# A decoder block's last projection as Strassen products, and raw reloads of plain weight blocks

## The chip, the cores and the metric

The kernel runs on one NeuronCore of a Trainium2 chip. The metric is the device time of one execution in microseconds (us). A core has five engines with queues of their own: TensorE (PE in the profile, with PEld for its weight loads), VectorE (DVE), ScalarE (ACT), GpSimd (POOL) and SyncE (SP), which here only issues DMAs. Each queue is worked off in order; engines wait for each other through semaphores. Matmuls read SBUF and add into PSUM banks of 128 x 512 float32; DVE and ACT read PSUM, POOL is used on SBUF alone.

## The reference: what is computed

One layer of a decoder block on 2048 tokens of width 1024, all in float32 (cut):

```python
h = rms_norm(x, g_norm) * (1 + scale) + shift          # scale, shift, gate from c
proj = h @ w_in                                        # 1024 x 8192
x_rnn, z_rnn, q, k, v, z_attn, g_r, g_a = split(proj)
y_rnn  = (rg_lru(conv(x_rnn)) * silu(z_rnn)) @ w_out_rnn
y_attn = (dilated_attention_mixture(rope(q), rope(k), v) * silu(z_attn)) @ w_out_attn
merged = sigmoid(g_r + b_r) * y_rnn + sigmoid(g_a + b_a) * y_attn
x = x + gate * (merged @ w_o)
return rms_norm(x, g_final)
```

The last projection is `merged @ w_o`, 2048 x 1024 times 1024 x 1024, followed by the residual add and the last norm.

## The kernel before

**Split operands.** Every product in float32 is made of three matmuls in a rounded 32-bit format. An operand is split into a high half (a copy that rounds, `hi_act` on ACT, line 157) and a low half (the difference, `lo_pool` on POOL, line 163, or `lo_dve` on DVE, line 166), and `mm3` (line 151) adds high x high, high x low and low x high. All matmuls stand at line 149; the profile tells them apart by the tile they write.

**The input stage.** Tokens are handled in two halves, f = 0 and 1, of 1024 tokens. For each half the value projections come first, then 28 pairs of weight column blocks, each by Strassen's scheme: a 256-column block of weights (two column tiles, two halves of K: left blocks a11, a12, a21, a22) times 1024 tokens (right operands B11, B21, B22, T1 to T4, each a high and a low tile of 128 x 4 x 512) takes seven products instead of eight. A product is 12 matmuls of 128 x 512 (4 K tiles x 3). In `strassen` (line 347) they go in the order B11, [the last of the pair before], T2, T3, T1, B21, T4, B22, into the PSUM tiles X, Z, W, V, Y. Sums of blocks run through `u1`, `u2`, `u3`. What happens between products is written out by product number: `operand_events` (line 262) loads the four raw blocks to R tiles (five slots), forms sums and differences on DVE and splits seven operands into S tiles (seven slots), each four products ahead (`LEAD`, line 260). In half 0 all 28 x 7 = 196 split operands are also stored to the scratch sD from ACT's DMA queue (line 275), two splits after they are made; in half 1 `load_next` (line 311) reads them back, 512 KB each, seven ahead. The whole stage is in program order.

**Pools.** Tiles of a stage lie in a pool; when a pool is closed and the next opened at its place, a new tile waits for those that lay where it lies. `rp` holds the tiles of the recurrent branch, of gates and of plain pairs, `qp` those of the last six pairs with the rotary turn; `xp` those with which the next half's operands are prepared meanwhile (`next_norm`, `next_even`, lines 1274 and 1297; `build`, line 514, makes one K tile of a right operand with a work tile hf). `rotary_tables` (line 1005) computes sine and cosine tables in some 18 small DVE steps, one after each product from `TABLES` on, and the four pieces at `PIECES`.

**Attention and output projections.** From about 1411 us on attention runs head by head, and its gaps are filled with steps of the two branch projections. `steps` (line 1708) is a generator of eight jobs: four token blocks of 512 through w_out_rnn, then four through w_out_attn. A job has 8 tiles (128 output rows), a tile 8 steps, a step three matmuls into a pj tile (two PSUM buffers). Within a tile stand the load of the next weight blocks (`load_w`, from split weights in the scratch wD, or, after `whole` is set, raw and split at once), the eviction of the tile before (`evict`: times the sigmoid gate on DVE from PSUM, for the attention jobs plus the other branch's part, line 1770 and 1772), the loads of its gate blocks into fg tiles (four slots), the store to mrT or meT, and in the last tile of a job the loads and splits of the next job's eight y blocks (`load_y`, `split_y`; blocks 1 to 4 through four R tiles). Six jobs are run inside the stretch written out in program order (line 1866); jobs 6 and 7, the ones that need the last heads, follow after it.

**The last projection.** There the program's planner sets the order, from its own estimate. Job 6's 64 steps come first in program text; then `output_operands` (line 1879) loads w_o, multiplies it by the residual gate and splits it into oh and ol; then `output(n)` (line 1887) for each block of 128 tokens loads x and merged (mraw), splits merged (mh, ml), makes 2 x 24 matmuls into pq tiles, adds x, squares and scales the row and stores it, one DMA of 512 KB. Between the blocks eight steps of job 7 are placed.

Of the kernel before, what the change touches and what calls it, by code (L numbers as in the profile page):

```python
# [10 lines left out]
F32 = mybir.dt.float32  # L11
# [15 lines left out]
H = 8  # L27
# [11 lines left out]
TABLES = 24  # L39
PIECES = (56, 76, 91, 111)  # L40
# [49 lines left out]
def decoder_block(ctx, tc, x, c, positions, g_norm, w_mod, b_mod, w_in, b_gate, conv_w, conv_b,  # L90
# [239 lines left out]


# [15 lines left out]
    def strassen(up, f, key, done):  # L347

        x = pair_id[key]
        if f and x == 0:  # L350
            while n_loaded[0] < NS:
                load_next()
        n_op = iter(range(7 * x, 7 * x + 7))
# [7 lines left out]
        def prod(ps, b, first, last, op=None):  # L361
# [6 lines left out]
            if f:  # L368
                used.add(i)
                while n_loaded[0] - NS in used:  # L370
                    load_next()
            run_late(n_prod[0])
# [138 lines left out]
    def n_hf(st):  # L511
        return 1 if st is xp else 2

    def build(st, names, xs, k, first=False, keep=None, pt=None):
# [7 lines left out]
        if keep is not None or first:  # L522
            hf = keep if keep is not None else T(st, [P, CH], F32, "hf", bufs=n_hf(st))[:]
# [5 lines left out]
        else:  # L529
            hf = T(st, [P, CH], F32, "hf", bufs=n_hf(st))  # L530
# [318 lines left out]
    def second_values():  # L849
# [5 lines left out]
        for i in range(4):  # L855
# [8 lines left out]
            plan[7, i].append(lambda i=i: [load_next() for _ in range(4 if i == 0 else 1)])  # L864
        plan[1, 0].append(lambda: ss.append(squares(x3)))
# [139 lines left out]
    def rotary_tables(rp, f):  # L1005
# [70 lines left out]
        at_, base = TABLES, n_prod[0]  # L1076
        for fn in (angles, None, products, *reduce(TWO_PI * 4096, 7, 8), *reduce(TWO_PI, 11, 5), quarter, sines):
            if fn:
                after_prod.setdefault(base + at_, []).append(fn)
            at_ += 1  # L1080
# [216 lines left out]
    def next_even():  # L1297
# [4 lines left out]
        def make(k):  # L1302
            if k % KH == 0:
                operand("B21" if k else "B11")
            build(xp, ("B11", "B21"), x0, k, pt=px.pop(k))
# [9 lines left out]


# [4 lines left out]
    for f in range(2):  # L1321
# [8 lines left out]
        rp = pools.open("rp", bufs=1)  # L1330
        plain_pool[0] = rp
# [21 lines left out]
        touch = [T(qp, [P, CH], F32, tag, bufs=n) for tag, n in (("t0", NT0), ("t1", NT1), ("u1", 1), ("u2", 2), ("u3", 1))]  # L1353
# [351 lines left out]
    stored, whole = set(), []  # L1705


    def steps(jobs):
# [4 lines left out]
        def load_w(x):  # L1713

            if x < 2 * len(tiles):
                assert x == n_w[0]
                j, m = tiles[x // 2]
                if not whole:
# [3 lines left out]
                n_w[0] += 1  # L1722
                W[x] = T(pS, [P, 2, KH, P], F32R, f"S{x % 4}")
                t = T(whole[0], [P, KH, P], F32, "wr", bufs=3)
                rows = slice(x % 2 * KH * P, (x % 2 + 1) * KH * P)
                nc.sync.dma_start(t[:], (w_out_rnn, w_out_attn)[jobs[j][0]][0, rows, m * P : (m + 1) * P]
# [225 lines left out]
```

## Time and profile before

| | |
|---|---|
| median of three runs | 2271.21 us (2270.94 to 2274.93) |
| the profiled execution | 2274.52 us, its span 2272.7 us |
| busy, share of the span | PE 98%, PEld 82%, DVE 61%, ACT 54%, POOL 44% |
| input stage, half 1 (838 to 1411 us) | PE 572.7 of 573.0 us busy |
| from job 6's first matmul to the end | 1989.6 to 2272.7 us |

The span is what the profile covers, from the first to the last instruction; the execution's own time has a little around it. A group of instructions is listed as line, engine, operation, output <- inputs by tile names, shapes and count, then busy us and mean ns of one, then idle time before them and what ended it. A matmul's own length in such a row (about 390 ns) is longer than the distance between two starts, since matmuls are pipelined; the cost per matmul is therefore read from the distance of starts.

### The profile page before, as it was taken

The page shows a single profiled execution, that of the slowest core. Times are in us where ns is not written, and L with a number is a line of the kernel's source. Part 1 is how long each engine was busy: PE and PEld are TensorE (multiplying, and loading weights), DVE is VectorE, ACT ScalarE, POOL GpSimd, SP SyncE. Part 2 cuts the span into 40 slices and gives each one's busy share as a digit, 9 for nine tenths or more (in the row PEclk, how much of TensorE's full clock was granted, in tenths as well). Part 3 has the DMA queues.
Part 4 walks back from the last instruction along what each step waited for, and adds up shares of the span by engine and source line. Part 5 has one row for each costly group of instructions (what it writes and reads, how often), then busy time and mean ns, then how long its engine had stood idle before and what let it go on. Part 6 is the DMA issues. An engine that isn't in the chain of part 4 may idle for free.

```text
span 2272.7 us, 34029 instructions
## 1 busy us (share of the span) xinstructions
PE 2220.0 (98%) x11454; PEld 1864.4 (82%) x11455; DVE 1382.2 (61%) x2384; ACT 1230.5 (54%) x2397; POOL 990.9 (44%) x738
## 2 busy tenths in 40 slices
PE   8999999999998999999999999999999999989998
PEld 5997788888777997888888887888889898868887
DVE  5568887767557465544444343466677878666443
ACT  3546777667542436655556411567778877533211
POOL 2268677766566343212222111456566666332100
PEclk9999999999999999999999999999999999999999
DMA  8366887887998448887887999989988897898542
GB/s 281 89 200 244 278 299 251 291 279 248 305 302 262 153 146 288 271 272 265 278 271 256 303 328 328 284 271 270 283 273 264 233 277 230 251 322 270 155 131 91
DMA packets 429011, 573.40 MB, mean 252 GB/s; under 512 B 72134, under 2 KB 293026, under 8 KB 427812
## 3 DMA queue, kind: packets, MB, share of 16 engines
q1 hardware_dynamic: 390996, 451.47, 64.4%
q10 hardware_dynamic: 37648, 119.70, 13.7%
q8 instruction: 91, 1.49, 0.3%
q14 instruction: 84, 0.69, 0.1%
q0 software_dynamic: 192, 0.05, 0.0%
HBM read 357.18 MB, written 213.91 MB: 251 GB/s over the span
## 4 chain that ended last, share of the span: by engine, by line
PE 59%; DMA 6%; DVE 3%; ACT 2%; SPq 2%; issue 1%; POOL 1%; ACTq 0%; POOLq 0%; DVEq 0%
PE pj L149 12%; PE X L149 8%; PE pq L149 8%; PE V L149 8%; PE W L149 4%; PE Z L149 4%; PE sc L149 4%; PE o L149 4%; PE Y L149 3%; DMA R<-in_w_in_dram 2%; PE pT L1555 1%; PE pg L149 1%; PE pT L1568 1%; DMA R<-yaT 1%; SPq L252 1%
## 5 line engine op out<-in xcount | busy, mean ns | idle before, releaser
L149 PE MATMUL pj<-yh,S 128*128 128x512 f32 x1024 | 344.7, 397 | 9.0 <-ACT S L157 5.3
L149 PE MATMUL V<-T,S 128*128 128x512 f32 x1344 | 332.6, 396 | 5.8 <-DVE t L449 2.6
L149 PE MATMUL X<-T,S 128*128 128x512 f32 x1344 | 332.6, 396 | 3.7 <-ACT u L382 1.9
L163 POOL TENSOR_TENSOR S<-R,S 128x512 fp32r<-128x512 f32 x168 | 252.7, 1512 | 166.8 <-ACT S L157 145.6
L149 PEld LDWEIGHTS V<-T,S 128*128 128x128 f32 x1344 | 253.4, 189 | 66.9 <-DVE ev L449 2.7
L149 PEld LDWEIGHTS X<-T,S 128*128 128x128 f32 x1344 | 254.0, 189 | 64.9 <-ACT u L382 2.4
L149 PEld LDWEIGHTS pj<-yh,S 128*128 128x128 f32 x1024 | 194.4, 190 | 49.8 <-ACT S L157 6.1
L149 PE MATMUL pj<-yl,S 128*128 128x512 f32 x512 | 202.3, 395 | 2.1 <-DVE yl L166 1.1
L163 POOL TENSOR_TENSOR S<-s,S 128x512 fp32r<-128x512 f32 x84 | 131.3, 1564 | 128.6 <-ACT S L157 95.5
L1471 ACT ACTIVATE pp<-pp,st 128x256 f32<-128x256 f32 (+3 forms) x256 | 133.4, 523 | 74.4 <-DVE st L1470 74.1
L149 PE MATMUL Y<-T,S 128*128 128x512 f32 x672 | 166.5, 397 | 0.0
L149 PE MATMUL W<-T,S 128*128 128x512 f32 x672 | 165.8, 395 | 0.0
L149 PE MATMUL Z<-T,S 128*128 128x512 f32 x672 | 165.8, 395 | 0.0
L163 POOL TENSOR_TENSOR s<-R,s 128x512 fp32r<-128x512 f32 x32 | 43.9, 1372 | 250.2 <-ACT s L157 205.8
L149 PEld LDWEIGHTS Y<-T,S 128*128 128x128 f32 x672 | 127.3, 190 | 29.7
L149 PEld LDWEIGHTS W<-T,S 128*128 128x128 f32 x672 | 126.0, 188 | 29.9 <-DMA kT<-t 0.9
L149 PEld LDWEIGHTS Z<-T,S 128*128 128x128 f32 x672 | 126.3, 188 | 29.4
L166 DVE TENSOR_TENSOR ptl<-pT,pth 128x384 fp32r<-128x384 f32 (+1 forms) x160 | 97.8, 628 | 51.1 <-ACT pth L157 48.9
L944 DVE SCALAR_TENSOR_TENSOR xc<-xr,par,xc 128x512 f32<-128x512 f32 x96 | 96.1, 1001 | 50.0 <-ACT xc L938 47.8
L1470 DVE CUSTOM_DVE_ANT_0 pp<-sc,msk 128x256 f32<-128x256 f32 (+3 forms) x256 | 104.2, 449 | 36.3 <-PE sc L149 34.1
L1535 ACT ACTIVATE pp<-pp,M 128x256 f32<-128x256 f32 (+3 forms) x256 | 118.1, 524 | 9.2 <-DVE M L1659 9.2
L163 POOL TENSOR_TENSOR kq<-kraw,kq 128x512 fp32r<-128x512 f32 (+1 forms) x64 | 101.2, 1592 | 41.7 <-ACT kq L157 32.1
(333 smaller groups left out, 4767.7 us busy)
## 6 DMA issues: line engine op xcount, KB each, us to landing
sD<-S ACTq DMA_DIRECT2D x196, 512.0 KB, 4.0
S<-sD SPq DMA_DIRECT2D x196, 512.0 KB, 4.8
S<-wD SPq DMA_DIRECT2D x99, 512.0 KB, 6.3
R<-in_w_in_dram SPq DMA_DIRECT2D x136, 256.0 KB, 4.0
wD<-s ACTq DMA_DIRECT2D x64, 256.0 KB, 4.9
T<-in_w_mod_dram SPq DMA_DIRECT2D x8, 1024.0 KB, 12.1
vN<-ev SPq DMA_DIRECT2D x64, 128.0 KB, 2.0
zaT<-ev SPq DMA_DIRECT2D x32, 256.0 KB, 4.6
```

What stands on the lines that cost most here:

```text
L149: nc.tensor.matmul(o, lhsT=l, rhs=r, start=st, stop=sp, **kw)
L163: nc.gpsimd.tensor_tensor(o, i, h.bitcast(F32), ALU.subtract)
L166: nc.vector.tensor_tensor(o, i, h.bitcast(F32), ALU.subtract)
L252: nc.sync.dma_start(t[:, :, o : o + src.shape[1]], src[half * KH * P : (half + 1) * KH * P].rearrange("(k p) m -> p k m", p=P))
L944: nc.vector.scalar_tensor_tensor(xc, xr[:, i : i + CH], cw(i), xc, ALU.mult, ALU.add)
L1470: nc.vector.tensor_tensor_reduce(pdst, s_ps, mask, 1.0, 3e38, ALU.add, ALU.min, m_)
L1471: nc.scalar.activation(pdst, pdst, AF.Exp, bias=m_, scale=-1.0, accum_out=l_)
L1535: nc.scalar.activation(pp, pp, AF.Copy, scale=w)
L1555: nc.tensor.transpose(pt[:, c0 + j * P : c0 + (j + 1) * P], pp[i][:, k * P : (k + 1) * P], ident)
L1568: nc.tensor.transpose(pt[:, c * P : (c + 1) * P], pp[:, half * P : (half + 1) * P], ident)
```

## The change

1. **The last projection by seven products.** `output_products` takes the place of `output_operands` and `output`. The right operands B11, B21, B22, T1 to T4 are made of the gated w_o: w_o comes in K tiles, and for each of four K indices a `group` of 2 gate products, 4 differences and 3 low halves on DVE, 7 high halves on ACT and 4 low halves on POOL is placed at numbered steps of jobs 6 and 7. The left side is merged, two 128-token blocks at a time (eight pairs): four raw loads from meT, four sums or differences, seven splits, issued `LEAD` products ahead, with S and R slots that jobs 6 and 7 leave. Evictions add into the x rows, partly on POOL (`add_x`), squares and scaling go in halves of 512 columns, one and two products later.
2. **Jobs 6 and 7 in program order.** All of it now lies inside the stretch in program order. Weight blocks from number 99 (`RAW_W`) on come raw into three slots, loaded four half tiles ahead (`u + 4`) and split two ahead (`split_w`); y blocks 5 to 7 of both jobs go through R tiles and are loaded in the first steps of the last tile before; the store of a tile is issued at step 5 instead of 7.
3. **Plain left blocks not stored.** The operands 0, 4 and 5 of a pair are the blocks a11, a12 and a22 themselves. For the 26 pairs whose columns come in fewer than 8 pieces they are no longer stored to sD; in half 1 they are loaded raw (256 KB) and split again, ACT and POOL, four products ahead (`split_next`).
4. **Placing in the input stage.** The table steps are spread, two to seven products, from product 32 on, the pieces later; `touch` claims the u tiles first in `rp` and `qp`, so that they lie at the same place in both; the work tile of `build` in `next_even` is one of three t1 tiles instead of a single hf.

```diff
-TABLES = 24
-PIECES = (56, 76, 91, 111)
+TABLES = 32
+PIECES = (117, 124, 131, 138)
...
+    PLAIN = {0: (0, 0), 4: (0, 1), 5: (1, 1)}
+    loaders, unsplit = {}, []
...
+        if len(pieces) < H:
+            loaders[x] = load
...
-            kept.append((7 * x + i, t))
+            if i not in PLAIN or x not in loaders:
+                kept.append((7 * x + i, t))
...
-            nc.sync.dma_start(t[:].bitcast(F32), sD[n])
+            if n % 7 in PLAIN and n // 7 in loaders:
+                unsplit.append((n, t, loaders[n // 7](*PLAIN[n % 7])))
+            else:
+                nc.sync.dma_start(t[:].bitcast(F32), sD[n])
...
+    def split_next(n):
+        while unsplit and unsplit[0][0] <= n:
+            _, t, r = unsplit.pop(0)
+            hi_act(t[:, 0], r)
+            lo_pool(t[:, 1], r, t[:, 0])
...
-            hf = T(st, [P, CH], F32, "hf", bufs=n_hf(st))
+            hf = T(st, [P, CH], F32, "hf", bufs=2) if st is vx else T(st, [P, CH], F32, "t1", bufs=NT1)
...
-                after_prod.setdefault(base + at_, []).append(fn)
-            at_ += 1
+                after_prod.setdefault(base + TABLES + 7 * (x // 2) + 2 * (x % 2), []).append(fn)
...
+        touch(rp, (("u1", 1), ("u2", 2), ("u3", 1), ("xc", 2), ("y", 2), ("gi", 1), ("a", 1), ("t", 1)))
...
+        touch(qp, (("u1", 1), ("u2", 2), ("u3", 1), ("t0", NT0), ("t1", NT1)))
...
+        def split_w(x):
+            if RAW_W <= x < 2 * len(tiles):
+                t = raw_w.pop(x)[:]
                 W[x] = T(pS, [P, 2, KH, P], F32R, f"S{x % 4}")
+                hi_act(W[x][:, 0], t)
+                (lo_dve if x % 2 else lo_pool)(W[x][:, 1], t, W[x][:, 0])
...
-                if k in (1, 2, 3, 4):
+                if k in (1, 2, 3, 4) or j >= LAST_HEAD and k:
                     load_yd(ys, n, k)
...
+                u = 2 * t + k // KH
                 if k % KH == 1:
-                    load_w(2 * t + k // KH + 3)
+                    for x in range(n_w[0], min(u + (4 if u + 3 < RAW_W else 5), 2 * len(tiles))):
+                        load_w(x)
+                    split_w(u + 2)
...
-                if k == 7 and t:
+                if k == (7 if j < LAST_HEAD else 5) and t:
                     store(t - 1)
...
+            return ((0, gate(0)), (1, gate(1)), (3, hi("B11", b11)), (4, hi("B22", b22)), (4, sub(t3, b22, b12)),
+                    (5, lo("B11", b11, lo_pool)), (6, hi("T3", t3)), (7, lo("B22", b22, lo_pool)),
+                    (7, sub(b12, b12, b11)), (9, hi("T1", b12)), (9, lo("T3", t3, lo_pool)), (10, sub(b22, b22, b12)),
+                    (11, hi("B21", b21)), (12, lo("T1", b12, lo_dve)), (13, hi("T2", b22)),
+                    (13, lo("B21", b21, lo_pool)), (16, lo("T2", b22, lo_dve)), (18, sub(b21, b21, b22)),
+                    (20, hi("T4", b21)), (22, lo("T4", b21, lo_dve)))
...
+        for k, (a, b, g) in enumerate(((4, 7, 16), (20, 30, 42), (40, 64, 72), (69, 85, 94))):
+            at_step(a, lambda k=k: load_o(k))
+            at_step(b, lambda k=k: load_o(KH + k))
+            at_step(g, lambda k=k, g=g: [at_step(g + d, fn) for d, fn in group(k)])
...
+        for x in range(len(order)):
+            X = T(pf, [P, CH], F32, "X", bufs=2)
+            product(X, "B11", True, False, 7 * x)
+            while held:
+                held.pop()()
+            Z = T(pf, [P, CH], F32, "Z")
+            product(Z, "T2", True, True, 7 * x + 1)
+            u1 = T(gp, [P, CH], F32, "u1", bufs=1)
+            u2 = T(gp, [P, CH], F32, "u2", bufs=2)
+            nc.scalar.activation(u1[:], X[:], AF.Copy)
+            tt(u2[:], Z[:], u1[:], ALU.add)
+            add_x(x, 0, 1, u2)
+            Wp = T(pf, [P, CH], F32, "W")
+            product(Wp, "T3", True, True, 7 * x + 2)
+            u3 = T(gp, [P, CH], F32, "u3", bufs=1)
+            tt(u3[:], Wp[:], u2[:], ALU.add)
+            add_x(x, 1, 1, u3)
+            add_x(x, 1, 0, u3)
+            V = T(pf, [P, CH], F32, "V")
+            product(V, "T1", True, False, 7 * x + 3)
+            finish(x, 1, 1, V, u3)
+            product(X, "B21", False, True, 7 * x + 4)
+            finish(x, 0, 0, X, None)
+            Y = T(pf, [P, CH], F32, "Y")
+            product(Y, "T4", True, True, 7 * x + 5)
+            finish(x, 1, 0, Y, u3)
...
-    spend(fill, KT * KT, 0)
-    output_operands()
-
-    for n in range(NB):
-        for _ in output(n):
-            for _ in range(KT):
-                next(fill, None)
+        pools.close("ap", "sc", "pT", "po")
+        output_products(fill)
```

More of the change, by code (lines that the diff above doesn't have):

```diff
@@ L522, in build @@
         if keep is not None or first:
[L523 removed]
+            hf = keep if keep is not None else T(st, [P, CH], F32, "hf", bufs=2)[:]
             if keep is None or k < KH:
@@ L1717, in load_w @@
                 j, m = tiles[x // 2]
-                if not whole:
+                if x < RAW_W:
                     load_wd(jobs[j][0], m, x % 2)
```

220 lines of the change are left out of this document (162 added, 58 removed).

## The prediction

> **What bounds the kernel now.** I read the page first, then the stages of the last 283 us, the chain in order of time, and what TensorE (PE) waited for.
>
> ```profile
> span 2272.7 us, 34029 instructions
> PE 2220.0 (98%) x11454; PEld 1864.4 (82%) x11455; DVE 1382.2 (61%) x2384; ACT 1230.5 (54%) x2397; POOL 990.9 (44%) x738
> ```
>
> PE is busy for 98% of the span, so time is won only by fewer matmuls or fewer waits of PE. The stages, columns as in the view (length, then busy us and instructions of PE, its weight loads, DVE, ACT, POOL, then granted clock, DMA share, GB/s); the first row counts only matmuls into pj:
>
> ```profile
> 1411.00:1989.60 578.60, 286.16 (x1152) 210.19 (x1153) 32.13 (x47) 1.00 0.87 264
> ```
> ```profile
> 838.00:1411.00 573.00, 572.69 (x2466) 462.17 (x2467) 258.30 (x358) 268.51 (x407) 126.51 (x96) 1.00 0.87 285
> ...
> 1989.60:2009.20 19.60, 11.71 (x37) 8.49 (x35) 5.94 (x8) 3.04 (x5) 2.54 (x2) 0.82 1.00 326
> 2009.20:2264.50 255.30, 255.23 (x1116) 210.43 (x1116) 131.90 (x214) 66.68 (x105) 39.60 (x21) 0.99 0.60 188
> 2264.50:2272.70 8.20, 0.00 (x0) 0.00 (x0) 2.91 (x8) 1.35 (x3) 0.00 (x0) 0.73 0.16 64
> ```
>
> Six of the eight projection jobs have 6 x 192 = 1152 matmuls, so the two last ones start at 1989.6. From there to the end are 283.1 us: 384 matmuls of jobs 6 and 7 (counted from 0) and 768 of the last projection, 1152 in all. What one costs, from the chain in order of time (start, length, what):
>
> ```profile
> 1364.65 2.79 PE Y L149 x12
> ...
> 2079.37 10.89 PE pq L149 x48
> 2090.26 5.45 PE pj L149 x24
> ```
>
> 48 in 10.89 and 24 in 5.45 are 0.227 us each; in the input stage's products 12 take 2.79, or 0.2325. So the 283.1 us are 1152 x 0.227 = 261.5 of PE work, 8.2 behind the last matmul, and 13.4 lost, nearly all between 1989.6 and 2009.2 (37 matmuls, 8.4 us of work, in 19.6).
>
> What PE waited for, the rows that matter here (us in total, times, longest):
>
> ```profile
> PE pj L149 <- ACT S L157: 5.3, 1, 5.3
> PE pg L508 <- DVE hf L531: 4.3, 2, 2.6
> ...
> PE pj L149 <- ACT yh L157: 2.6, 1, 2.6
> PE V L149 <- DVE t L449: 2.6, 3, 1.8
> ...
> PE V L149 <- DVE ev L449: 2.3, 1, 2.3
> PE X L149 <- ACT u L382: 1.9, 1, 1.9
> ...
> PE X L149 <- DMA S<-sD: 1.8, 2, 1.5
> ```
>
> **The last projection.** Sixteen row blocks times 48 matmuls become eight pairs times seven products of 12: 672 instead of 768. The time of a product lies between 12 x 0.227 = 2.72 and 2.79. I take 2.79, because that row is the same instruction pattern (a split block stationary, a four-part right operand moving): 56 x 2.79 = 156.2 instead of 768 x 0.227 = 174.3, a gain of 18.1 (21.8 at the other end).
>
> The other engines must keep up with that. Durations from the groups by line and shape (after the bar: busy us, mean ns of one), first of the whole run, then of the stretch from 1990 on:
>
> ```profile
> L163 POOL TENSOR_TENSOR S<-R,S 128x512 fp32r<-128x512 f32 x168 | 252.7, 1512 | 166.8 <-ACT S L157 145.6 <-DMA R<-in_w_in_dram 8.4 <-issue 6.3
> ...
> L157 ACT ACTIVATE S<-R 128x512 fp32r<-128x512 f32 x168 | 102.1, 620 | 20.2 <-DMA R<-in_w_in_dram 12.2 <-DVE R L292 3.5 <-DMA kT<-t 2.5
> ...
> L283 DVE TENSOR_TENSOR s<-R,R 128x512 f32<-128x512 f32 x28 | 32.6, 1163 | 10.5 <-DMA qT<-t 6.9 <-DMA R<-in_w_in_dram 3.6
> ```
> ```profile
> L163 POOL TENSOR_TENSOR S<-wr,S 128x512 fp32r<-128x512 f32 x14 | 24.3, 1737 | 81.2 <-ACT S L157 72.7 <-DMA wr<-in_w_out_attn_dram 8.5
> ...
> L1910 DVE SCALAR_TENSOR_TENSOR ob<-xo,ss,gf 128x1024 f32<-128x1024 f32 x16 | 20.6, 1284 | 0.6
> L1908 ACT ACTIVATE ob<-xo 128x1024 f32<-128x1024 f32 x16 | 16.8, 1050 | 28.7 <-DVE xo L1905 27.8 <-DMA out_dram<-ob 0.8
> ...
> L1772 DVE TENSOR_TENSOR fg<-fg,fg 128x512 f32<-128x512 f32 x17 | 16.2, 953 | 1.1 <-DMA fg<-mrT 1.0
> ...
> L166 DVE TENSOR_TENSOR S<-wr,S 128x512 fp32r<-128x512 f32 x15 | 13.4, 894 | 5.4 <-ACT S L157 5.3
> L1770 DVE TENSOR_TENSOR fg<-pj,fg 128x512 f32<-128x512 f32 x17 | 11.7, 687 | 9.6 <-PE pj L149 8.1 <-DMA mraw<-meT 0.8 <-DMA fg<-gaT 0.7
> ...
> L1883 DVE TENSOR_TENSOR xo<-xo,gate_b 128x1024 f32<-128x1024 f32 x8 | 10.3, 1301 | 1.9 <-DMA xo<-in_w_o_dram 1.8
> ```
>
> Per pair (19.5 us of PE): POOL 7 low halves and 3 adds of x, 10 x 1.51 = 15.1; DVE 4 sums x 1.16, 6 PSUM adds x 0.69, 4 half-width scalings x 0.64 and some 2 us of one-column steps, 13.4; ACT 7 x 0.62 and about 4 more. Each fits. POOL's adds wait for u2 and u3, so for PE, and the splits behind them wait with them; but a split is queued four products (11 us) ahead. I take 2 us for the first pair, whose x rows and fifth to seventh split slots come only after job 7's memory is free (0 to 8).
>
> **Jobs 6 and 7 in program order.** PE work stays 384 x 0.227 = 87.2. Counting what DVE and POOL get in these 87 us. DVE: 16 evictions x (0.687 + 0.953) = 26.2; 20 low halves of weights and y x 0.894 = 17.9; four operand groups, each two gate products, four differences and three low halves, 4 x (2.6 + 4.65 + 2.68) = 39.7; three sums for the first pair, 3.5: 87.3 in all. POOL: 14 weight low halves x 1.737 and 24 others x 1.512, 60.6. The groups start at step 16 of 128; before it stand some 11 us of work, so 137 fall into the remaining 76.2 us of PE, 90 per 50 us. Have they ever gone so densely? The busiest 50 us of the input stage:
>
> ```profile
> 200.00:250.00 50.00, 47.70 (x198) 37.70 (x197) 45.06 (x49) 36.15 (x58) 34.60 (x23) 0.97 0.70 250
> 250.00:300.00 50.00, 50.00 (x217) 40.55 (x216) 41.54 (x53) 37.30 (x61) 36.68 (x25) 1.00 0.86 287
> ...
> 600.00:650.00 50.00, 48.05 (x201) 38.60 (x200) 15.04 (x24) 15.22 (x27) 20.56 (x15) 0.97 1.00 304
> ```
>
> DVE and POOL together reach 78.2 per 50 with PE always busy, and 79.7 with PE waiting 2.3. At 78.2 the 137 take 87.6 us, 11.4 too many. PE tolerates an eviction one tile late (5.4 us, two PSUM buffers), but of that the gate load eats some 2: it is issued 3.4 us before its tile ends and lands after
>
> ```profile
> meT<-fg SPq DMA_DIRECT2D x9, 256.0 KB, 5.5
> fg<-gaT SPq DMA_DIRECT2D x9, 256.0 KB, 5.1
> fg<-mrT SPq DMA_DIRECT2D x8, 256.0 KB, 5.6
> ```
>
> leaving 3.2. So 8 us of PE waiting, and 2 more because everything is queued in program order (a high half on ACT that waits for a late DVE difference holds up the next weight block behind it): 10. The lower end is 0: DVE's 87.3 alone just fit. The upper end, from rows of undisturbed and disturbed lengths (min/median/max ns):
>
> ```profile
> L163 POOL TENSOR_TENSOR S<-wr,S x14: 1278/1682/2347, 2010.1 to 2142.8; 128x512 fp32r<-128x512 f32 x14
> ```
> ```profile
> L166 DVE TENSOR_TENSOR S<-wr,S x15: 677/693/1785, 2009.2 to 2145.5; 128x512 fp32r<-128x512 f32 x15
> ```
>
> The same DVE subtraction lasts 0.68 or 1.79, and 1.79 is 0.68 and most of one POOL subtraction: where both read two SBUF operands, one stands while the other runs. If that is complete, their undisturbed lengths add up: 36 on POOL x 1.278 = 46.0, 34 on DVE x 0.677 = 23.0, groups 4 x (2 x 1.3 + 7 x 0.677) = 29.4: 98.4 for 76.2, less 3.2: 19.0. I keep 10, by the row of 250 to 300, which is the nearest mixture. The Trainium skill, page "SBUF — State Buffer", section "Who interferes with whom", says that a VectorE instruction with two SBUF inputs and a GpSimd one that reads SBUF exclude each other for a whole instruction. The trace agrees in kind (1.79 against 0.68); by the rule to the letter the sum would have 19.0 here.
>
> A second road to the same wait are the transfers. The four fg buffers turn in load 5.6, add 1.0, store 5.5 and issues 0.5, 12.6 us for two tiles that PE does in 10.9; SP stands at the load that needs the slot, and the next weight load stands behind it. That the store is issued two steps earlier gives back 1.4. And the bytes: 29 raw weight blocks, 32 gate blocks, 16 stores, 10 y blocks and 4 left blocks of 0.26 MB, with 4.7 of w_o and its gate, are 28.6 MB; the stage from 1989.6 moved 326 GB/s at a full DMA share, which makes 88 us of it. Both lie inside the same 0 to 19 and are not added.
>
> **The start of job 6.** Today it loses 11.2 us: y blocks loaded late (2.6), the first raw weight block split late (5.3), the rest half clock. Now y 5 to 7 are loaded in job 5's last tile, and a raw block is loaded four half tiles ahead (10.9 us) and split two ahead. The y loads still wait for the slots of y 1 and 2, so I leave 2 us (0 to 11).
>
> **The end.** 8.2 becomes 7.5: square and scaling go at half width (0.5 of the 1.05 saved; the two scalings still follow each other), and the last store is 256 KB (bounds 6.5 and 8.2).
>
> **The front.** In the stage of 838 to 1411 the 78 plain blocks (26 pairs, three each) come raw, 256 instead of 512 KB, and cost 78 x 0.62 on ACT and 78 x 1.51 on POOL: ACT goes to 317 and POOL to 244 of 573 us, both covered by PE. An ACT high half waits for its load, and PSUM copies queue behind it; it is queued three products (8.4 us) after the load, which takes
>
> ```profile
> S<-sD SPq DMA_DIRECT2D x196, 512.0 KB, 4.8
> ...
> R<-in_w_in_dram SPq DMA_DIRECT2D x136, 256.0 KB, 4.0
> ```
>
> so 0, at most 5. In the first half 78 stores of 512 KB go; the rest are issued later, since two kept blocks stay behind, and the worst (block 3) only two products, 5.6 us, before its slot is written again, against 4.0 to landing:
>
> ```profile
> sD<-S ACTq DMA_DIRECT2D x196, 512.0 KB, 4.0
> ```
>
> 0, at most 3, ACT standing. The stalls named above: DVE's table steps, one per product (the 2.3 at V, half clock after it: 0.97 over 50 us is 1.5), are spread over seven products for every two: 3.8. The u copy that stood behind a store of the closed pool,
>
> ```profile
> 619.03 0.60 ACT L382 ACTIVATE u<-X 128x512 f32<-128x512 f32 x1 [7.94 <-DMA gaT<-ev]
> ```
>
> now gets a u tile's place: 1.9 and half clock (0.97 in the row of 600 to 650 above), 3.4. Of the 4.3 at hf (three buffers instead of one) I take 2, since ACT stood behind late loads there too; of V behind t 1, of S from sD 1.2. Minus 0.4 for new waits: 11 (3 to 17). What is late next near 619 and 659 are the many-piece loads of the rotated blocks, which stay.
>
> **The sum.** From 1989.6: 87.2 + 2 + 10 + 156.2 + 2 + 7.5 = 264.9 against 283.1, 18.2 less; with 11 in front 29.2 less: span 2243.5. The profiled execution took 2274.52 with a span of 2272.7, the median is 2271.21; so 1.5 below the span, 2242.
>
> **Rivals.** (1) DVE and POOL keep up in jobs 6 and 7 because part of the lag is worked off in the product phase: stall 0, 2232. For it: DVE alone fits. Against: 90 per 50 us has no precedent. (2) They exclude each other fully: 19.0 instead of 10, 2251. (3) Slower: POOL becomes the bound of the product phase. Its 15.1 us per pair are synchronised with PE twice (u2, u3); if a pair took it 24 us instead of 19.5, eight pairs would add 36, 2278. It decides from 23.2 us per pair (29.2 / 8 above 19.5). Against: between u3 and the next u2 lie six products, 16.7 us, for eight POOL operations of 12 us.
>
> **Numbers.** Forecast 0.47, rival 1 0.27, rival 2 0.18, rival 3 0.06, no change 0.02 (0.2%, 4.5 us, is about what a measurement tells). Best ends (stall 0, 2.72, front 17) give 2222; rival 2 with the front at 3 gives 2259, with late first pairs 2262. Range 2222 to 2262. Faster 0.92, same 0.02, slower 0.06.
>
> **What would show it.** 672 matmuls into X, Z, W, V, Y after job 7, 2.79 a product; PE waits in jobs 6 and 7 on DVE's fg or the weight halves, about 10 us, with DVE over 90% busy there; no PE wait behind u at line 382 near 619. Wrong if PE waits on S or POOL in the product phase, or on S in the second half of the input stage.

## The result, and the profile after

| | before | after |
|---|---|---|
| median | 2273.36 us (9 runs) | 2280.71 us (9 runs) |
| ratio | | 1.0036, 95% interval 1.0023 to 1.0049 |
| profiled execution, its span | 2274.52, 2272.7 us | 2277.73, 2275.7 us |

The change made the kernel 0.36% slower; 1.3% faster was forecast. From the page of the changed kernel:

```profile
span 2275.7 us, 34368 instructions
PE 2210.1 (97%) x11358; PEld 1848.6 (81%) x11359; DVE 1485.9 (65%) x2472; ACT 1301.8 (57%) x2575; POOL 1223.6 (54%) x908
```

The 96 matmuls are gone and PE is busy for 9.9 us less, yet the span is 3.0 us longer. The stages of the changed kernel from the end of the input stage on (same columns as in the prediction): attention with jobs 0 to 5, jobs 6 and 7, the products, and what lies behind the last matmul.

```profile
1400.20:1977.20 577.00, 564.88 (x3553) 502.06 (x3552) 398.01 (x1101) 409.91 (x1093) 324.33 (x279) 1.00 0.87 266
1977.20:2090.00 112.80, 96.62 (x386) 73.80 (x385) 90.97 (x93) 40.80 (x70) 58.96 (x38) 0.95 0.88 264
2090.00:2266.20 176.20, 163.38 (x672) 129.91 (x671) 125.36 (x206) 59.30 (x139) 109.71 (x78) 0.96 0.44 138
2266.20:2275.70 9.50, 0.42 (x2) 0.00 (x0) 5.24 (x17) 0.93 (x3) 0.00 (x0) 0.65 0.29 110
```

Job 6 starts at 1977.2, where it started at 1989.6: 12.4 us are won in front, 11 were forecast. Against the sum of the prediction, the loss in jobs 6 and 7 is 112.8 - 87.2 = 25.6 instead of 12 (13.6 more), the products take 176.2 instead of 158.2 (18.0 more), the end 9.5 instead of 7.5 (2.0 more); with 1.4 more won in front that makes the 32.2 us between 2243.5 and 2275.7. What PE waited for (us in total, times, longest), first in jobs 6 and 7, then in the product phase:

```profile
PE pj L149 <- DVE S L166: 4.0, 5, 1.5
PE pj L149 <- DMA S<-wD: 3.1, 1, 3.1
PE pj L149 <- DVE yl L166: 2.9, 3, 1.8
PE pj L149 <- DVE fg L1794: 2.5, 2, 1.5
PE pj L149 <- POOL yl L163: 1.4, 1, 1.4
...
```
```profile
PE V L149 <- DVE xo L2000: 12.8, 8, 2.4
```

In the product phase there is one wait only: for V, the PSUM tile that the last product of a pair leaves to DVE's add into the x rows (line 2000). The order of time shows it in a long pair and in the short one behind it (start, length, what, idle before):

```profile
2115.65 2.96 PE L149 MATMUL W<-F,S 128*128 128x512 f32 x12
2121.02 4.46 PE L149 MATMUL V<-F,S 128*128 128x512 f32 x12 [2.42 <-DVE xo L2000]
...
2139.29 2.96 PE L149 MATMUL W<-F,S 128*128 128x512 f32 x12
2143.16 3.04 PE L149 MATMUL V<-F,S 128*128 128x512 f32 x12 [0.90 <-DVE xo L2000]
```

A wait of 2.42 us is followed by half clock here all four times (granted clock 0.50 from 2123 to 2125 us; 4.46 instead of 3.04 for twelve matmuls), one of 0.90 is not, and so the pairs alternate: by the starts of Z, 20.1, 23.6, 20.6, 23.6 us and so on. It is no fixed rule: in copies_no_gates, one of the runs below, a wait of 2.58 us leaves the granted clock at 1.00. And what DVE itself waited for in these 176.2 us, the four costliest:

```profile
DVE ss L2013 <- ACT jk L2011: 19.7, 15, 1.9
DVE xo L2000 <- POOL xo L2032: 9.7, 8, 1.4
DVE s L1944 <- DMA R<-meT: 7.7, 1, 7.7
DVE u L2045 <- ACT u L2044: 5.3, 7, 0.8
```

DVE is busy for 125.4 us and stands for 42.4 more at these four, which is 95% of the stage: it hardly ever waits for PE. The 7.7 are a single wait, at the first pair's raw blocks; the others come back with every pair. Its queue is a closed chain of work and of waits for ACT and POOL, and PE runs at that chain's pace.

### The profile page after: what moved, and what is told of

Same layout as the page of the kernel before. It is cut to its first block, busy times and chain, and to the rows that moved or that the text cites. A ratio compares the mean times of both kernels' runs of the same rounds, so it can differ in the third digit from the quotient of the medians.

```text
span 2275.7 us, 34368 instructions
## 1 busy us (share of the span) xinstructions
PE 2210.1 (97%) x11358; PEld 1848.6 (81%) x11359; DVE 1485.9 (65%) x2472; ACT 1301.8 (57%) x2575; POOL 1223.6 (54%) x908
## 5 line engine op out<-in xcount | busy, mean ns | idle before, releaser
L163 POOL TENSOR_TENSOR S<-R,S 128x512 fp32r<-128x512 f32 x278 | 412.7, 1491 | 364.8 <-ACT S L157 318.7
L157 ACT ACTIVATE S<-R 128x512 fp32r<-128x512 f32 x278 | 170.7, 622 | 137.0 <-DMA R<-in_w_in_dram 91.3
L163 POOL TENSOR_TENSOR S<-s,S 128x512 fp32r<-128x512 f32 x112 | 165.9, 1481 | 131.8 <-ACT S L157 99.1
L149 PEld LDWEIGHTS Z<-T,S 128*128 128x128 f32 x672 | 126.6, 188 | 29.7
L149 PEld LDWEIGHTS Y<-T,S 128*128 128x128 f32 x672 | 126.6, 188 | 29.3
L157 ACT ACTIVATE S<-s 128x512 fp32r<-128x512 f32 x117 | 73.0, 624 | 126.4 <-issue 33.4
L1489 DVE CUSTOM_DVE_ANT_0 pp<-sc,msk 128x256 f32<-128x256 f32 (+3 forms) x256 | 104.1, 448 | 36.4 <-PE sc L149 34.2
```

Source lines behind the costliest of these rows:

```text
L149: nc.tensor.matmul(o, lhsT=l, rhs=r, start=st, stop=sp, **kw)
L157: nc.scalar.activation(o, i, AF.Copy)
L163: nc.gpsimd.tensor_tensor(o, i, h.bitcast(F32), ALU.subtract)
L1489: nc.vector.tensor_tensor_reduce(pdst, s_ps, mask, 1.0, 3e38, ALU.add, ALU.min, m_)
```

## The product phase: order, and what DVE and POOL keep from each other

**V in two banks.** Is it the single bank of V, or the chain?

```diff
-            V = T(pf, [P, CH], F32, "V")
+            V = T(pf, [P, CH], F32, "V") if x % 2 == 0 else T(pj, [P, CH], F32, "pj")
```

> The changed kernel; the V tiles of the odd pairs take the PSUM bank that job 7 leaves (a tile named pj), so that two V tiles exist at a time. In the changed kernel PE waits 12.8 us, eight times, at V for the add into xo (line 2000), and four of these waits are followed by half clock; the phase from 2090.0 to 2266.2 takes 176.2 us where 56 products are 156.2. Theory A (order): DVE has time enough, the add only stands behind norm steps in its queue, and one bank is all that makes PE feel it: the waits go, the pairs take 19.6 us each, the phase 156 to 159, the kernel 18 to 20 us less than the changed one. Theory B (throughput): DVE and POOL together need 20.6 us or more per pair; the wait only moves, to Z, X or a split operand S, and the phase stays above 165, the gain under 11 us.

Measured: 2280.29 us, ratio to before 1.0035 (1.0021 to 1.0048), the same as without the edit. All pairs from the second on are 22.1 to 22.2 us apart; after's mean is 176.2 / 8 = 22.0. What PE waits for has moved:

```profile
PE X L149 <- ACT u L2044: 10.0, 7, 1.5
PE pj L149 <- DVE xo L2000: 3.4, 4, 1.1
PE V L149 <- DVE xo L2000: 2.3, 3, 0.8
```

```profile
2087.90:2262.60 174.70, 159.06 (x673) 125.03 (x671) 125.22 (x206) 59.20 (x139) 109.58 (x78) 1.00 0.45 139
```

The half clock is gone (granted clock 1.00 in the phase), and the phase is 1.5 us shorter, no more. So neither the bank nor the half clock is the cause; theory A falls as it was put, and the chain has a period of 22.1 us.

**Adds first.** The seven calls that put the next operands' work on the queues go behind the adds of each product:

```diff
             done_n[0] += 1
-            run_jobs(done_n[0])
...
             finish(x, 1, 1, V, u3)
+            run_jobs(done_n[0])
```

> The changed kernel; in the product phase the adds behind a product (into u or xo) are put on the queues ahead of the next operands' sums and splits and of the norm steps, which were ahead of them. V stays one bank. Theory A (order): the add into xo that frees V then runs some 2 us behind the last product of a pair, 3 us before V is wanted, and u3 and POOL's adds of x come earlier as well: the phase takes 156 to 160 us instead of 176.2, the kernel 16 to 20 us less than the changed one. Theory B (throughput of DVE and POOL): the operands come late instead, PE waits on S, and the phase stays above 165.

Measured: 2267.72 us, 0.9976 (0.9965 to 0.9988). The phase, and what DVE waited for most in it:

```profile
2091.50:2256.30 164.80, 158.16 (x673) 125.23 (x672) 126.59 (x204) 57.55 (x138) 106.78 (x78) 1.00 0.48 148
```
```profile
DVE ss L2012 <- ACT jk L2010: 17.2, 7, 2.5
DVE s L1945 <- POOL S L163: 7.1, 6, 1.2
```

The phase is 164.8 us, the pairs 21.0 from the third on: 11 of the 20 lost us were order alone. That lies between the two theories, above A's 156 to 160 and just under B's 165. The waits of DVE for POOL's add of x and for ACT's copy are gone from its list; left are the two shown.

**Fewer low halves on POOL.**

```diff
                 hi_act(t[:, 0], v[name])
-                lo_pool(t[:, 1], v[name], t[:, 0])
+                (lo_pool if i % 2 else lo_dve)(t[:, 1], v[name], t[:, 0])
```

> The kernel with the adds ahead (evict_first: pairs of 21.0 us, phase 164.8), and in the product phase four of a pair's seven low halves (operands 0, 2, 4, 6) on DVE instead of POOL. Theory A (DVE and POOL exclude each other while both read two SBUF operands, and that sum is the limit): per pair 10 POOL operations x 1.28 and 8 such DVE operations x 0.68 are 18.2 us of 19.5, and a low half costs 1.28 on POOL but 0.68 on DVE, so four moved leave 15.8: pairs of 19.6 to 20.0, the phase 157 to 160. Theory B (DVE's own queue is the limit): DVE, busy for 15.8 us a pair, gets 2.7 more, and the pairs stay at 21 or grow, the phase 165 or more.

Measured: 2263.71 us, 0.9959 (0.9944 to 0.9973). The stage:

```profile
2094.90:2253.20 158.30, 156.42 (x673) 125.95 (x672) 138.19 (x237) 57.66 (x139) 72.35 (x47) 1.00 0.49 155
```

158.3 us, which is what the prediction had for it (158.2). DVE got 31 operations of 0.68 more, 21 us, and is busy for only 11.6 more than with the adds first alone (138.2 against 126.6 in 164.8): its other operations became shorter by the rest (the sum at line 1944, for one, 0.68 us on average instead of 1.21). Theory A's numbers hold, B falls. What the run doesn't separate is POOL's lateness: with the adds first alone DVE waited 7.1 us and PE 1.8 for a low half from POOL, and these waits are gone too. Where the prediction's "some 2 us of one-column steps" went shows in the groups of the changed kernel's product phase (busy us, mean ns of one) and, for the step at line 176, in its order of time behind POOL's last instruction:

```profile
L176 DVE TENSOR_TENSOR ss<-ss 128x1 f32<-128x1 f32 x14 | 15.1, 1076 | 0.5
...
L177 DVE TENSOR_TENSOR ss<-ss 128x1 f32<-128x1 f32 x14 | 9.6, 688 | 0.5
...
L170 DVE TENSOR_SCALAR ss<-ss 128x1 f32<-128x1 f32 x14 | 2.2, 154 | 0.5
```
```profile
2267.46 0.16 DVE L176 TENSOR_TENSOR ss<-ss 128x1 f32<-128x1 f32 x1
...
2268.23 1.41 DVE L2020 SCALAR_TENSOR_TENSOR xo<-xo,ss,gf 128x512 f32<-128x512 f32 x2
```

The step at line 176 takes 0.16 us where POOL is idle and 1.08 on average in the phase, that at line 177 0.69. Both multiply two columns from SBUF. The steps with one column as input (lines 170, 175 and 178) take 0.15 us every time. Line 179 also has two, and takes 0.16: POOL is idle when it runs (in the first long pair POOL's last low half ends at 2118.43 us and line 179 begins at 2118.67). All seven kinds of one-column steps together take 42.9 us, some 5 a pair.

## Jobs 6 and 7: two losses that add

**POOL's low halves as copies on ACT** (weights, y and the four of a group that are POOL's; `lo_copy` is a copy by ACT):

```diff
-                (lo_dve if x % 2 else lo_pool)(W[x][:, 1], t, W[x][:, 0])
+                (lo_dve if x % 2 else lo_copy)(W[x][:, 1], t, W[x][:, 0])
```

> The changed kernel with the 38 low halves that POOL makes in jobs 6 and 7 (weights, y, operand groups) replaced by copies on ACT: these low halves are not computed. DVE keeps every instruction. From job 6's first matmul to job 7's last the changed kernel takes 112.8 us for 87.2 of PE work; DVE is busy for 91.0 of it, and its subtractions last 0.68 or 1.77 us. Theory A (DVE and POOL exclude each other): all of DVE's subtractions fall to 0.68, DVE's busy time to about 74, and the 25.6 lost us to 5 to 9, of which some 4.4 are the late weight block at the start. Theory B (the order of the queues, or the transfers): DVE's durations fall but PE still waits for fg and S, and 18 or more are still lost. Theory C (DVE's own work alone is too much): also 18 or more lost, with DVE busy over 85.

Measured: 2270.46 us (one execution). The same DVE subtraction in the changed kernel and here, ns min/median/max:

```profile
L166 DVE TENSOR_TENSOR F<-wo,F x12: 679/1766/1785, 2005.9 to 2083.8; 128x512 fp32r<-128x512 f32 x12
```
```profile
L166 DVE TENSOR_TENSOR F<-wo,F x12: 683/685/1781, 2005.5 to 2076.5; 128x512 fp32r<-128x512 f32 x12
```

and the stretch:

```profile
1978.40:2082.50 104.10, 94.68 (x385) 75.57 (x384) 64.44 (x92) 58.01 (x105) 3.41 (x3) 0.93 0.93 284
```

With POOL silent they take 0.68; the one of 1.78 begins at 2076.5, 0.1 us behind the first low half of the product phase, which POOL still makes. And DVE's busy time falls from 91.0 to 64.4. By the Trainium skill, page "SBUF — State Buffer", section "Who interferes with whom", a VectorE instruction with two SBUF inputs contends with a GpSimd instruction that reads SBUF; the trace agrees, down to steps of one column with two inputs. But the stretch is 104.1: 8.7 us are won and 16.9 still lost, between theory A's 5 to 9 and theory B's 18. Some of that may belong to the edit, which makes ACT busy for 58.0 us instead of 40.8: PE waits 2.2 us for an operand from ACT. A single execution can be read here: the three kernels of the section above have jobs 6 and 7 as in the changed kernel (product_lows but for the first pair's splits), and their stretches are 113.0, 112.9 and 112.0 us.

**Without the gate loads.** 

```diff
-            for src in (grT,) if ys is yaT else (gaT, mrT):
+            for src in (grT,) if ys is yaT else (gaT, mrT) if j < LAST_HEAD else (mrT,):
```

> As pool_lows_as_copies (POOL's low halves of jobs 6 and 7 not computed; 104.1 us for the stretch, 16.9 of it lost), and the sigmoid gate blocks of jobs 6 and 7 are not loaded: a tile is multiplied by the other branch's block and a constant tile is added instead, the same two DVE instructions. So 16 transfers of 256 KB go, and the four fg slots serve four tiles instead of two. Theory A (what is left of the loss is transfers: a gate block that lands after its tile has ended, behind a store that holds its slot): the stretch is 91 to 94, with the late weight block at the start as the only wait of PE. Theory B (the order of the queues): 99 or more.

Measured: 2261.25 us (one execution). The stretch, and the longest of PE's waits in it:

```profile
1981.60:2076.40 94.80, 89.17 (x384) 71.33 (x383) 64.41 (x92) 57.79 (x105) 4.55 (x3) 1.00 0.86 271
```
```profile
PE pj L149 <- DMA S<-wD: 2.6, 1, 2.6
```

94.8 us, 0.8 over theory A's range: 9.3 of the 16.9 were the gate blocks, with their slots and the 16 transfers that SP and the DMA no longer have. What is left waits for the last split weight block at the start of job 6 and for y at the start of job 7.

**Without the operand groups.** ACT copies raw blocks of w_o into both halves:

```diff
-            return ((0, gate(0)), (1, gate(1)), (3, hi("B11", b11)), (4, hi("B22", b22)), (4, sub(t3, b22, b12)),
...
+            return ((3, hi("B11", b11)), (4, hi("B22", b22)), (5, lo("B11", b11)), (6, hi("T3", b22)),
...
```

> The changed kernel with the operand groups' work of jobs 6 and 7 left out: no gate products, no differences, no low halves; ACT copies raw blocks of w_o into both halves. Weights and y are split as in the changed kernel, their low halves on DVE and POOL in turn. Theory A (the groups are what overloads DVE and POOL): the stretch, 112.8 us in the changed kernel, is 92 to 98. Theory B (program order, raw weight blocks and late gate blocks lose time by themselves): 103 or more.

Measured: 2263.80 us (one execution); the stretch is 103.4, in theory B's range. The stretch, and what DVE waited for:

```profile
1973.80:2077.20 103.40, 93.61 (x384) 73.96 (x383) 45.02 (x57) 53.93 (x98) 29.66 (x22) 0.95 0.93 287
```
```profile
DVE fg L1794 <- DMA fg<-gaT: 25.5, 13, 6.0
```

DVE is now busy for 45 of 103 us, and stands 13 times, up to 6.0 us, at a gate block that has not landed. The groups bring 9.4 of the 25.6 lost us, much the same share that POOL's low halves brought (16 of which are theirs, so the two shares overlap); 16.2 stay with the program order and its late loads, and with ACT's copies.

**More on DVE, and more gate slots.** Thirty of POOL's 38 low halves go to DVE (all of the weights and of y, T3 and B21):

```diff
-                (lo_dve if x % 2 else lo_pool)(W[x][:, 1], t, W[x][:, 0])
+                lo_dve(W[x][:, 1], t, W[x][:, 0])
...
```

> The changed kernel; in jobs 6 and 7 thirty of the 38 low halves that POOL makes go to DVE (all of the weights and of y, and T3 and B21 of the operand groups; B11 and B22 stay). With POOL's low halves as copies the stretch took 104.1 us and DVE was busy for 64.4. Theory A (exclusion): DVE gets 30 x 0.68 = 20.4 and some 5 for the eight that stay, 90 in all and about what it is busy now, but nothing waits for POOL any more: the stretch is 104 to 107, the kernel 6 to 9 us under the changed one. Theory B (DVE's work is the limit): 112 or more.

Measured: 2274.55 us, 1.0012 (0.9996 to 1.0028); the stretch is 107.6, 5.2 us less than in the changed kernel, DVE busy for 87.1. That is 0.6 over theory A's stretch, and by the ratios some 5.5 us under the changed kernel where A had 6 to 9; B's 112 is far off. The same work is faster with nearly all of it on DVE than shared with POOL. And, on the changed kernel, six gate slots:

```diff
-            wo[k] = T(fp, [P, D], F32, "wo", bufs=3)
+            wo[k] = T(fp, [P, D], F32, "wo", bufs=2)
...
+                if k == 6 and LAST_HEAD * KT <= t < len(tiles) - 1:
+                    load_g(t + 1)
```

> The changed kernel with six gate slots instead of four in jobs 6 and 7 (the third tile of w_o gives them up) and gate blocks loaded at step 6 of the tile before, 6.8 us instead of 3.4 ahead of their use; operand groups at steps 16, 45, 74 and 103. Nothing is taken from DVE or POOL. Theory A (late gate blocks and the lock between DVE and POOL add up): the stretch falls from 112.8 to 102 to 107. Theory B (they lie inside the same wait, as the prediction had it; DVE is late anyway): 110 or more.

Measured: 2285.35 us, 1.0062 (1.0040 to 1.0084), the stretch 118.5: worse. DVE waits less for gate blocks and what is added to them (7.6 us instead of 12.9), but 4.9 us for w_o, whose third tile was given up, and PE now waits 9.2 us for split weights (POOL 3.4, DVE 3.1, ACT 2.7), where it waited 6.2. The edit moved the groups and took a w_o tile as well, so it does not say what earlier gate loads are worth by themselves; that stays open.

## The front: which part brought it

front_alone is the kernel before with parts 3 and 4 of the diff. placing_only and stores_kept change one place each in it: the first reloads nothing raw, the second stores the plain blocks although it reloads them raw.

```diff
-    PLAIN = {0: (0, 0), 4: (0, 1), 5: (1, 1)}
+    PLAIN = {}
```
```diff
-            if i not in PLAIN or x not in loaders:
-                kept.append((7 * x + i, t))
+            kept.append((7 * x + i, t))
```

> The kernel before with parts 3 and 4 of the change only (plain blocks not stored, table steps spread, the u tiles claimed first, t1 instead of hf); jobs 6 and 7 and the last projection as before. In the changed kernel job 6 began 12.4 us earlier than in the kernel before (1977.2 against 1989.6). Theory: the front's gain is independent of the end, so job 6 begins near 1977, everything behind it keeps its 283.1 us, and the span is near 2260, 0.55% faster. Rival: the start of job 6 in the old order waits for transfers, not for PE, and gives some of it back: its 11.2 lost us grow, and the span is 2264 to 2270.

Measured: 2266.64 us, 0.9971 (0.9956 to 0.9985): by the ratio 6.6 us (3.4 to 10) of 2271.87. In the profiled executions of kernels with this same front job 6 starts anywhere between 1973.8 and 1984.7 (1982.4 here), so the 12.4 us of the one profile of after lie towards the good end. From there to the end front_alone takes 282.3 us, as the kernel before does (283.1): the end is independent, as the theory has it, and the rival's reason does not hold, although the span of 2264.7 lies in its range. It is the front that brought 7.2 us in this profile and not 12.4.

> front_alone without its raw reloads: all left blocks are stored and reloaded split, as before; the table steps spread, the u tiles claimed, t1 instead of hf. front_alone was 5 us faster than the kernel before. Theory A (prediction: the raw reloads cost and bring about nothing, all gain is from the placing): within 2 us of front_alone, 2264 to 2268. Theory B (fewer bytes are what helps): 2269 or more. Theory C (the 78 more splits on POOL and ACT cost what the placing gains): under 2263.

Measured: 2273.22 us, 1.0001 (0.9992 to 1.0009): nothing, theory B's range.

> front_alone with the stores of the plain left blocks put back: in the first half of the tokens all split operands go to the scratch as before (78 transfers of 512 KB more from ACT's queue), in the second half the plain ones are still loaded raw. front_alone was 5 us faster than the kernel before, placing_only equal to it. Theory A (the stores crowd the transfers between 560 and 760 us, where V waits for t behind late loads): as placing_only, 2270 to 2275. Theory B (the smaller reloads of the second half are what helps): as front_alone, 2264 to 2268.

Measured: 2278.55 us, 1.0015 (1.0006 to 1.0024). In kind that is theory A; it is even above A's 2270 to 2275, but the kernel before had a median of 2274.46 us in the runs beside it. So the whole gain of the front is the 78 stores that are not made (10 us between front_alone and stores_kept, by the ratios). The raw reloads by themselves seem to cost some 3 us (1.0015 against 1.0001, two intervals that just meet). In the profiles PE's waits for S tiles from 770 to 1411 us add up to 5.2 us in stores_kept, 1.5 in placing_only and 1.8 before.

The place is the one where the rotated pairs begin, 560 to 760 us. All waits of PE from 560 to 770 us add up to 9.7 us before, 9.1 in placing_only, 8.6 in stores_kept, 4.0 in front_alone and 3.0 in after: they fall where the stores are left out, and only there. What PE waited for there, the 40 us in which it happens, and the stores from ACT's queue over the 200 us (count, KB each, us to landing), first in placing_only:

```profile
PE V L149 <- DVE t L465: 5.2, 2, 4.8
```
```profile
640.00:680.00 40.00, 35.19 (x146) 28.16 (x145) 28.58 (x35) 17.20 (x31) 27.39 (x18) 0.96 0.94 290
```
```profile
sD<-S ACTq DMA_DIRECT2D x55, 512.0 KB, 4.1
```

and then in front_alone:

```profile
PE V L149 <- DVE t L465: 0.2, 1, 0.2
```
```profile
640.00:680.00 40.00, 39.83 (x172) 32.03 (x171) 31.17 (x41) 17.96 (x32) 27.26 (x18) 1.00 0.88 251
```
```profile
sD<-S ACTq DMA_DIRECT2D x38, 512.0 KB, 4.3
```

Seventeen stores fewer in these 200 us, and the wait of V for the rotation's t, 4.8 us and a stretch at a lower clock behind it, is gone. In stores_kept, with 55 stores again, it is back:

```profile
PE V L149 <- DVE t L464: 3.1, 2, 2.6
```

That t was late because what it is made from came late over a full DMA fits the traces; the chain from one store to one load was not followed.

## Put together

best_a is product_lows and lows_mostly_dve; best_c adds a fifth gate slot, gate loads a tile ahead and an eviction whose first product stays in PSUM; best_d is best_c with the y loads of the last tile before jobs 6 and 7 behind its gate load; best_e is best_a with that order of loads and nothing of best_c. The first cut below is best_c's eviction, the second the order of the y loads in best_d and best_e:

```diff
+            if tiles[t][0] >= LAST_HEAD:
+                nc.vector.tensor_tensor(ps[:], ps[:], g[0][:], ALU.mult)
+                nc.vector.tensor_tensor(g[1][:], ps[:], g[1][:], ALU.add)
+                return
...
-                    if k in (1, 2) and j + 1 >= LAST_HEAD:
-                        load_y(j + 1, k + 4)
-                    if k == 2 and j + 1 >= LAST_HEAD:
+                    if k in (3, 4) and j + 1 >= LAST_HEAD:
+                        load_y(j + 1, k + 2)
+                    if k == 4 and j + 1 >= LAST_HEAD:
```

> product_lows (adds first, four low halves a pair on DVE) and lows_mostly_dve (thirty low halves of jobs 6 and 7 on DVE) together. Theory A (each takes away a share of what DVE and POOL keep from each other, in its own stretch): they add, the stretch of jobs 6 and 7 is 105 to 108, the phase 158, the kernel 4 to 6 us under product_lows, near 2259. Theory B (what jobs 6 and 7 gain is given back at the first pair, whose operands come late): within 2 us of product_lows.

> best_a, and in jobs 6 and 7 the first product of an eviction stays in PSUM (the second instruction then reads one SBUF operand only), five gate slots instead of four, and gate blocks loaded at step 6 of the tile before. Theory A (with POOL out of the way late gate blocks are the wait that is left, as in the run without gate loads, 94.8 us): the stretch is 96 to 101, the kernel 6 to 10 us under best_a. Theory B (as in fg_six, earlier gate loads only push the weight blocks back): 105 or more.

> best_c with the loads of y blocks 5 to 7 of jobs 6 and 7 issued two steps later, behind the gate load of the last tile of the job before. Theory A (at the start of job 6 the gate block and the last split weight block land late because SP stands at the y loads in front of them): the first wait, 3 us and a half clock, goes, 3 to 5 us less than best_c. Theory B (the blocks are late because the last head's own transfers fill the DMA): no difference, or PE waits for y instead.

> best_a with the loads of y blocks 5 to 7 of jobs 6 and 7 behind the gate load of the last tile of the job before (as in best_d, but with four gate slots and the constants as they were). Theory A (the 5.4 us that PE waits for y at the start of job 6 are a gate load that stands behind the y loads): the stretch of jobs 6 and 7 falls from 110.3 to 103 to 106, the kernel to 2254 to 2258. Theory B (five slots are needed for it): as best_a, 2261.

| | us | ratio to before | jobs 6 and 7 |
|---|---|---|---|
| best_a | 2260.98 | 0.9948 (0.9929 to 0.9966) | 110.3 |
| best_c | 2258.64 | 0.9939 (0.9923 to 0.9955) | 109.0 |
| best_d | 2260.52 | 0.9946 (0.9933 to 0.9958) | 105.3 |
| best_e | 2256.06 | 0.9915 (0.9900 to 0.9930) | 103.8 |

best_a missed its 105 to 108, and its 2.5 us under product_lows (by the ratios) are nearer to theory B than to A's 4 to 6: PE now waits 9.9 us for y blocks at the starts of the two jobs. best_c missed its 96 to 101: DVE's waits for gate blocks fell from 9.8 to 5.4 us, but SP now stands 12.0 us in front of weight loads and 7.3 in front of w_o (9.0 and 2.8 in best_a). The order of the y loads shortened the stretch both times (109.0 to 105.3, 110.3 to 103.8), but best_d, with 3 to 5 us less forecast, is no faster than best_c as a whole; only best_e came out as theory A had it. best_e beats both kernels. Of its stages

```profile
1981.90:2085.70 103.80, 94.98 (x384) 72.23 (x383) 86.32 (x119) 40.87 (x70) 14.83 (x9) 0.97 0.92 281
2085.70:2245.20 159.50, 156.81 (x673) 125.89 (x673) 137.78 (x237) 57.71 (x139) 71.90 (x47) 1.00 0.49 154
2245.20:2255.30 10.10, 0.43 (x2) 0.00 (x1) 5.56 (x19) 1.02 (x4) 0.00 (x0) 0.72 0.27 104
```

the products are near where the prediction had them (159.5 against 158.2), and jobs 6 and 7 still lose 16.6, 4.6 more than it had. With the end (10.1 instead of 7.5) and the start of job 6 (7.7 us earlier than before instead of 11) that is the whole distance of 11.8 us between this span, 2255.3, and the 2243.5 of the prediction.

## Why the prediction was wrong, step by step

- **"Each fits" in the product phase: the step that failed, 18.0 us.** The sum of DVE's durations, 13.4 us of 19.5, was set against the length of a pair. DVE was busy for 15.7 a pair (125.4 / 8), the one-column steps taking some 5 instead of 2, and another 4.3 went into waits for ACT and POOL in the middle of its queue (19.7, 9.7 and 5.3 in all). Both were in reach: 1.79 against 0.68 was quoted for jobs 6 and 7 and not used for this phase, and the queue's order was not walked through. Rival 3 had the place and the period to which such a pair leads (24 us there, 22.0 here), at 0.06, but with the wrong engine: POOL is busy for 109.7 of 176.2 us and waits for DVE. So neither of the two signs of being wrong that were named for this phase came: PE waited neither for S nor for POOL, but at V for DVE.
- **The loss in jobs 6 and 7: the mechanisms right, the term too small, 25.6 instead of 12.** "Both lie inside the same 0 to 19 and are not added" is the step that failed. Without POOL's low halves 16.9 are lost, without the groups 16.2, without POOL's low halves and the gate loads 7.6: the exclusion (8.7) and the late gate blocks (9.3) add to 18.0 where 10 were booked for both, and 7.6 remain, mostly at the starts of the two jobs. The exclusion of rival 2 is there in kind (1766 ns against 685), but taking POOL's low halves away brought 8.7 us and not 19.0. Two signs came out otherwise as well: DVE is busy for 81% of the stretch and not for over 90%, and PE's waits add up to 16.1 us instead of about 10.
- **The start of job 6**: 2 us were left. Up to 1990.0, 12.8 us hold 37 matmuls (8.4 us of work), so 4.4 were lost, at the last split weight block; the bound of 11 held. The prediction named the slots that the y loads wait for. What it left out is that a gate load stands behind them in SP's queue: with that order changed, best_e's stretch is 6.5 us shorter than best_a's.
- **The front**: the size held in the profile (12.4 against 11) and was too high for the medians (6.6, inside 3 to 17). So the agreement in the profile is luck. The reason was wrong in the main: with the placing alone the 2.3 us at V are gone (PE is busy for 50.0 us from 200 to 250, where it was 47.7), but nothing is won in the end, because the waits between 560 and 770 us stay (9.1 instead of 9.7) in a stretch whose row showed a DMA share of 1.00. The stores, booked at 0, were the whole gain.
- **The product's price**: 2.79 was right; in product_lows PE is busy for 156.4 us over the 56 products.
- **The end**: 9.5 instead of 7.5. The last row's norm steps stand behind the two scalings of the row before (1.41 us on DVE at 2268.23), which comes at the same time now that rows end in pairs.
- **The range.** Its upper end, 2262, does not take the prediction's own upper bounds together: 19 in jobs 6 and 7, 11 at the start of job 6, 8 for the first pair, 8.2 at the end and 3 in front make 2275. With the product phase alone put right (product_lows, 158.3 us) the kernel runs 2263.71 us, at the edge of the stated range.

## What to carry to other kernels

Adding up an engine's durations tells whether it could keep up, not whether it does: on an in-order queue walk one period through, with every wait for another engine, before a period in which it is 70% busy is called covered. Where VectorE and GpSimd both read two SBUF operands, book both on one line and move work to the one that is shorter (0.68 against 1.28 us here), even if it looks the busier. And stores that nobody waits for are not free in a stretch whose DMA share is 1.00: 78 of them cost 10 us here, most likely by what they push back, the next loads.

## What the runs showed that was not expected

One-column VectorE steps with two SBUF inputs stretch as wide ones do beside GpSimd (0.16 to 1.08 us on average at line 176), and those with one input do not (0.15 each time). And in best_c and best_d, whose constants tile is 448 bytes smaller so that other tiles lie lower, a product of the input stage takes 2.80 us, where it takes 2.78 to 2.80, 2.79 on average, in kernels whose tiles were not moved (from 300 to 340 us in best_c and in product_lows). That would be about 2 us over the 200 products of a half; the cause was not followed up.
